# Filler products ahead of x, transposed blocks copied by ScalarE, and a later sum of blocks, in a hybrid attention layer on one core

## The chip, the core and the metric

The kernel runs on one core of a Trainium2 chip. The core has five engines, each with a queue of its own that it works off in order: TensorE (PE in the profile; its weight loads are listed apart as PEld), VectorE (DVE), ScalarE (ACT), GpSimd (POOL) and SyncE (SP), which here only issues DMAs. Matrix products leave their sums in one of eight PSUM banks of 128x512 numbers; everything else lies in SBUF or in device memory. Instructions wait for each other through semaphores. The metric is the device time of one execution in microseconds (us), the median of several runs.

## The reference

One layer: a norm of the input, one wide projection into nine parts, two groups of heads side by side, an output projection and a second norm.

```python
h = rms_norm(x, pre_g)                                  # x: 1024 x 1024
z = einsum('bsd,de->bse', h, w_in)                      # 7184 columns
qa, ka, va, ga, qb, kb, vb, gb, gk_low = split_columns(z)
# 8 heads: w = softmax(q1 k1^T) - lam * softmax(q2 k2^T), causal; oa = w v
oa = rms_norm(diff_attention(qa, ka, va, lam), subln_g) * (1 - lam_init) * silu(ga)
# 4 gated heads: S_t = diag(exp(log_a_t)) S_{t-1} + k_t^T v_t ; o_t = q_t S_t, in chunks
log_a = log_sigmoid(gk_low @ w_gk_up + b_gk) / 16
ob = rms_norm(gla_chunked(qb, kb, vb, log_a), gla_g) * silu(gb)
y = einsum('bse,ed->bsd', concatenate([oa, ob], -1), w_out)
return x + rms_norm(y, post_g)
```

All inputs and the output are float32.

## The kernel before

**Split numbers.** TensorE takes its operands in a shorter format (fp32r). Each operand is therefore split into a part `hi`, a rounded copy that ACT makes, and a part `lo`, the difference that DVE makes, and a product is three: hi by hi, hi by lo, lo by hi. So each block that TensorE is to use costs ACT one instruction and DVE one, and DVE comes last.

**Seven products for eight.** The normed input h is transposed and cut into a 2x2 grid of blocks, by tokens and by columns of x: `h11`, `h12` from the first 512 tokens, `h21`, `h22` from the last. A pair of projection columns is cut likewise into `b11` to `b22`. Seven block products then stand for eight. Products n = 1, 2 and 4 take the blocks h11, h12, h22; n = 5, 6, 7, 3 take the sums `s1` = h21 + h22, `s2` = s1 - h11, `s3` = h11 - h21 and `s4` = h12 - s2. In the code, `f1` holds whole copies of h11 and h12; s2 is written over the first, and s4 is taken from the second (`f1lo`) and the first (`f1hi`). Each block has four pieces j = 0..3 of 128x512. The weights of n = 5, 6, 4, 7 are differences of the b blocks, which DVE writes over the raw columns `w_raw`. One step (p, n) of the list `order` is one product for one pair of columns; `go(n)` issues the next n steps, and inside it `prepare` makes weights up to three steps ahead. Weights lie in a ring of five tiles, raw columns in four buffers: a load of new raw columns waits until the last reader of the old ones is done. A step leaves its sum in a bank named x, y or z, 24 products to a step in the first part.

**The start.** Eight 128-row tiles of x are loaded, the first four ahead. For each of these, ACT squares and sums it (`junk`), ACT and DVE work out the scale, DVE scales the first 512 columns and POOL the rest. `first(0)` transposes the first halves of the four tiles into four banks (`xT`), from which `put` makes h11; `first(1)` does it for h12. Tiles 4 to 7 are normed two at a time and scaled by POOL. `blocks(j)`, j = 0..3, transposes two more blocks of these and makes from them piece j of h22, s1, s2 and s3: ACT copies h21 and h22_hi out of the banks, and DVE reads the second bank twice more, for h22_lo and for s1. After them come four pieces of s4, four subtractions on DVE and their split. `low_rank` then prepares a small weight `wl2` and multiplies it with all blocks (`gkl_ps`); its gates are needed by later steps.

**Later.** The remaining steps of the projection run to the end of the list; between them the generator `gla(g)` places the work of the four gated heads, one piece at each `yield`: scores (`pa`, `pk`), states (`kv`), outputs (`gpo`), their sum of squares (`gms`), and the store. The last pairs (VALS) are the values of the attention heads; there two pieces are drawn to a step. Then come the attention heads, run against the output projection, and the end.

**What sets the order.** A scheduler of the framework orders each engine's queue by data and its own estimates, except where the code holds instructions in the order in which they are written (`keep_in_program_order`: every product and transpose, and some of the start) or ties them behind another (`issue_after`). Banks are handed out from a list `free`, oldest first; who takes a bank waits for its last readers.

The lines that the steps of the prediction touch are L117 (product), L120 (transpose), L333, L352 and L353 (weights: difference, hi, lo), L574 (squares), L604 and L605 (split from a bank), L623 and L625 (f1), L645 to L652 and L630, L631 (blocks), L721 (s4), L734 to L752 (low_rank), L462 (values).

## Time and profile before

| | us |
|---|---|
| median of 3 runs (lowest to highest) | 974.47 (974.18 to 975.09) |
| the profiled execution, its own time | 975.12 |
| its span, first to last instruction | 973.4 |
| TensorE busy | 952.3 (98%) |
| VectorE busy | 734.2 (75%) |
| ScalarE busy | 603.0 (62%) |
| GpSimd busy | 205.7 (21%) |

The profile is of one execution. The timeline gives for each group of like instructions the start, the busy time of the group, engine, line, operation, what it writes and reads, the shape and the count; a bracket at the end gives how long the engine stood idle before it, and what ended that. Instructions overlap at their ends, so the time that an engine gives to each is read from one start to the next and not from the busy time. Products are pipelined: 24 of the form 128x256 have busy times that overlap by much, and their rate is read from the starts. The table of stretches shows, after start:end and length, the busy time and count for PE, PEld, DVE, ACT and POOL, then the granted clock of TensorE and the traffic of the DMAs.

### The profile page before, as it was taken

What the parts mean: (1) busy time and instruction counts of PE and PEld (TensorE: products, weight loads), DVE (VectorE), ACT (ScalarE), POOL (GpSimd) and SP (SyncE); (2) the same over time, 40 slices, a digit from 0 to 9 for tenths busy, and PEclk for the clock granted to TensorE, in tenths of its full rate; (3) what the DMA queues carried; (4) which work ended last, traced back from release to release, by engine and by line L of the source; (5) the groups of instructions that cost most, each with busy time, mean ns of one, the idle gap of its engine ahead of it and who ended that gap; (6) DMA issues with size and microseconds to landing.
All of it is one profiled execution on the core that took longest, in us unless ns stands there. A gap on an engine that the chain in (4) does not pass through costs nothing.

```text
span 973.4 us, 15020 instructions
## 1 busy us (share of the span) xinstructions
PE 952.3 (98%) x4946; PEld 811.1 (83%) x4946; DVE 734.2 (75%) x1462; ACT 603.0 (62%) x1164; POOL 205.7 (21%) x263
## 2 busy tenths in 40 slices
PE   6999999999999999999999999999999999999997
PEld 5998988888888888888888888878888888888785
DVE  6887598897677686686766677487888888898554
ACT  8642454764667565576765344366786687887773
POOL 4300001212141221131100002121322222443322
PEclk9999999999999999999999999999999999999999
DMA  9443456478768987996854589997656759995777
GB/s 356 142 113 89 139 162 233 168 243 268 229 205 253 290 271 257 285 299 208 258 184 125 175 240 288 397 295 240 222 173 225 235 194 356 333 292 106 153 212 144
DMA packets 152301, 220.39 MB, mean 226 GB/s; under 512 B 16752, under 2 KB 87408, under 8 KB 152128
## 3 DMA queue, kind: packets, MB, share of 16 engines
q1 hardware_dynamic: 138128, 178.80, 57.5%
q0 software_dynamic: 14096, 40.64, 14.7%
q8 instruction: 39, 0.64, 0.3%
q14 instruction: 38, 0.31, 0.1%
HBM read 133.93 MB, written 88.60 MB: 229 GB/s over the span
## 4 chain that ended last, share of the span: by engine, by line
PE 93%; DVE 3%; ACT 1%; DMA 1%; issue 1%; POOL 0%; DVEq 0%; SPq 0%; ACTq 0%
PE x L117 24%; PE z L117 15%; PE y L117 14%; PE ypart L117 13%; PE sc L117 7%; PE po L117 5%; PE yps L117 4%; PE wtr L120 3%; PE gpo L117 3%; PE kv L117 1%; PE gkl_ps L117 1%; PE pa L117 1%; DMA v_raw<-in_w_in_dram 1%; PE xT L120 0%; ACT junk L574 0%
## 5 line engine op out<-in xcount | busy, mean ns | idle before, releaser
L352 ACT CAST w<-w_raw 128x512 fp32r<-128x512 f32 (+1 forms) x150 | 98.0, 655 | 90.1 <-PE y L117 46.9
L353 DVE TENSOR_TENSOR w<-w_raw,w 128x512 fp32r<-128x512 f32 (+1 forms) x150 | 109.4, 732 | 40.8 <-ACT w L352 40.4
L1148 ACT ACTIVATE p<-p,stt 128x896 f32<-128x896 f32 (+7 forms) x128 | 99.3, 777 | 36.5 <-DVE stt L1138 33.8
L510 ACT COPY s<-x 128x512 f32<-128x512 f32 x72 | 42.2, 586 | 74.7 <-PE x L117 74.2
L1154 POOL TENSOR_SCALAR p<-p,stt,lam 128x1024 f32<-128x1024 f32 (+3 forms) x64 | 56.2, 878 | 146.6 <-DVE stt L1153 144.9
L677 POOL DMA_DIRECT2D wo_d<-wo_hi x32 | 17.7, 552 | 328.6 <-ACT wo_hi L667 328.6
L1138 DVE CUSTOM_DVE_ANT_0 p<-sc,maskt 128x512 f32<-128x512 f32 (+3 forms) x128 | 74.3, 585 | 14.8 <-PE sc L117 13.5
L117 PE MATMUL z<-s_hi,w 128*128 128x512 f32 x320 | 80.2, 393 | 0.0
L117 PE MATMUL x<-s_hi,w 128*128 128x512 f32 x320 | 80.0, 392 | 0.0
L117 PE MATMUL y<-h_hi,w 128*128 128x512 f32 x320 | 80.0, 392 | 0.0
L117 PE MATMUL ypart<-wo_hi,m_hi 128*128 128x512 f32 x192 | 79.5, 414 | 0.1
L117 PE MATMUL ypart<-wo_hi,m_lo 128*128 128x512 f32 x192 | 75.5, 393 | 0.0
L117 PE MATMUL ypart<-wo_lo,m_hi 128*128 128x512 f32 x192 | 75.4, 393 | 0.0
L333 DVE TENSOR_TENSOR w_raw<-w_raw 128x512 f32<-128x512 f32 (+1 forms) x88 | 66.2, 752 | 9.3 <-DMA w_raw<-in_w_in_dram 8.2
L117 PE MATMUL sc<-k,q 128*128 128x512 f32 (+1 forms) x192 | 68.9, 363 | 1.2 <-DVE stt L1138 1.2
L117 PEld LDWEIGHTS z<-s_hi,w 128*128 128x128 f32 x320 | 59.7, 188 | 12.2
L117 PEld LDWEIGHTS y<-h_hi,w 128*128 128x128 f32 x320 | 59.7, 188 | 12.2
L117 PEld LDWEIGHTS x<-s_hi,w 128*128 128x128 f32 x320 | 59.7, 188 | 12.2
L117 PE MATMUL sc<-ks,q 128*128 128x512 f32 (+1 forms) x192 | 66.1, 347 | 0.0
L1196 ACT CAST wt_hi<-wtr 128x512 fp32r<-128x512 f32 (+1 forms) x80 | 42.8, 535 | 25.3 <-PE wtr L120 24.4
L1197 DVE TENSOR_TENSOR wt_lo<-wtr,wt_hi 128x512 fp32r<-128x512 f32 (+1 forms) x80 | 50.6, 633 | 9.1 <-ACT wt_hi L1196 8.4
L1157 DVE SCALAR_TENSOR_TENSOR p<-p,stt,p 128x1024 f32<-128x1024 f32 (+3 forms) x64 | 52.1, 814 | 4.1 <-POOL p L1154 3.8
(236 smaller groups left out, 2323.5 us busy)
## 6 DMA issues: line engine op xcount, KB each, us to landing
w_raw<-in_w_in_dram SPq DMA_DIRECT2D x48, 512.0 KB, 4.6
wo_d<-wo_hi POOLq DMA_DIRECT2D x32, 256.0 KB, 3.3
q<-q_d SPq DMA_DIRECT2D x32, 256.0 KB, 5.1
k<-k_d SPq DMA_DIRECT2D x32, 256.0 KB, 5.6
ks<-k_d SPq DMA_DIRECT2D x64, 128.0 KB, 6.0
v<-v_d SPq DMA_DIRECT2D x16, 512.0 KB, 7.1
wo_raw<-in_w_out_dram POOLq DMA_DIRECT2D x31, 256.0 KB, 4.9
wo_d<-gqd POOLq DMA_DIRECT2D x22, 256.0 KB, 4.1
```

The lines of the kernel that those rows point to most:

```text
L117: tc.keep_in_program_order(pe.matmul(*a, **k))
L120: tc.keep_in_program_order(pe.transpose(dst, src, ident))
L333: dve.tensor_tensor(dst, a, b, ALU.subtract)
L352: act.copy(w[0], src)
L353: dve.tensor_tensor(w[1], src, fp(w[0]), ALU.subtract)
L510: act.copy(b[k], ps)
L1138: ins = dve.tensor_tensor_reduce(p[:, a:e], sc[:, : e - a], maskt[:, NZ + P - (e - a) :] if last else maskt[:, : e - a], 1.0, 3e38 if i == ...
L1148: act.activation(p[:, :n], p[:, :n], AF.Exp, bias=st[:, m : m + 1], scale=-1.0, accum_out=st[:, 2 + m : 3 + m],)
L1154: pool.tensor_scalar(p1[:, :n], p1[:, :n], st[:, 5:6], lam, ALU.mult, ALU.mult)
L1157: dve.scalar_tensor_tensor(p0[:, :n], p0[:, :n], st[:, 4:5], p1[:, :n], ALU.mult, ALU.subtract)
L1196: act.copy(hi[:, :n], pt[:, :n])
L1197: dve.tensor_tensor(lo[:, :n], pt[:, :n], fp(hi[:, :n]), ALU.subtract)
```

## The change

Seven things are altered.

- The constants `ones` and a zeroed tile `idle` are made first on POOL. `spin(n)` multiplies the two n times into a bank that nobody reads. 14 such products stand ahead of the first transposes, and 3, 7, 3 and 4 behind the transposes of tiles 0 to 3.
- While `pinned` is set, ACT, DVE and POOL keep the written order too: it holds for the start, for the split of h11, for the norm of tiles 4 to 7, which is now written ahead of the first step, and for the copies of `blocks(0)`. The first four weights are tied by this in place of `issue_after`; weights 4 to n_early + 1 are tied behind the last pinned instruction.
- POOL's four additions for `f1[0]` come after the scaling of tiles 4 to 7.
- `blocks`: ACT copies h22 whole out of its bank into SBUF; hi, lo and s1 are made from that copy. The bank is read by ACT alone. For odd j the copy uses the buffer `t4`, which the first piece of w_out used from the start and now gets later.
- `blocks(j)` stands one step earlier among the steps, and s4 four steps later, its four subtractions tied behind DVE's latest instruction there.
- The multiplication of `sub_g` on DVE is held in the written order.
- In the last gated head's second half two of the three-`yield` delays are two `yield`s long.

```diff
@@ constants, queues
-    act, dve, pool, pe, sp = nc.scalar, nc.vector, nc.gpsimd, nc.tensor, nc.sync
+    pe, sp = nc.tensor, nc.sync
+    pinned = [False]
+
+    class Queue:
...
+            def run(*a, **k):
+                ins = op(*a, **k)
+                self.latest = getattr(ins, "ins", None)
+                if pinned[0]:
+                    tc.keep_in_program_order(ins)
+                    self.last = ins.ins
+                return ins
...
+    act, dve, pool = Queue(nc.scalar), Queue(nc.vector), Queue(nc.gpsimd)
...
+    ones = const.tile([P, P], F32R, name="ones")
+    pool.memset(fp(ones), 1.0)
+    idle = hw.tile([P, 512], F32R, tag="s1_hi0", name="idle")
+    pool.memset(fp(idle), 0.0)
...
-        if i < 4:
-
-            act_ins, dve_ins = normed[0][:2]
-            with tc.issue_after(act_ins.ins), tc.issue_after(dve_ins.ins):
+        if 4 <= i <= n_early + 1:
+            with tc.issue_after(act.last), tc.issue_after(dve.last):
                 make_weights(i)
...
+    spins = []
+
+    def spin(n):
+
+        if not spins:
+            spins.append(bank(free[-1], [P, 512], "spin"))
+        for i in range(n):
+            mm(spins[0], ones, idle, start=(i == 0), stop=(i == n - 1))
...
     def first(h):
 
         ps = [take_bank([P, 512], "xT") for _ in range(HB)]
+        if not h:
+            spin(14)
         for i in range(4):
             for j in range(HB):
                 k = h * HB + j
                 tr(ps[j][0][:, i * P : (i + 1) * P], xs[i][:, k * P : (k + 1) * P])
+            if not h:
+                spin((3, 7, 3, 4)[i])
         hi, lo = H[("h11", "h12")[h]]
         for j in range(HB):
             put(ps[j][0], h * HB + j, (hi, lo), j)
+        pinned[0] = not h
+        for j in range(HB):
             if h:
                 act.activation(f1[h][:, j], ps[j][0], AF.Copy, scale=pre_g[:, h * HB + j : h * HB + j + 1])
-            else:
-                pool.tensor_tensor(f1[h][:, j], fp(at(hi, j)), fp(at(lo, j)), ALU.add)
             free.append(ps[j][1])
...
         k = j + HB
+        pinned[0] = not j
         h21 = t_c("h21")
+        h22 = ap.tile([P, 512], F32, tag="t4", name="h22", bufs=1) if j % 2 else t2k("s", 4, "h22")
         act.activation(h21, pss[0], AF.Copy, scale=pre_g[:, j : j + 1])
-        put(pss[1], k, block("h22"), j)
+        act.activation(h22, pss[1], AF.Copy, scale=pre_g[:, k : k + 1])
         s1 = t_c("s1")
-        dve.scalar_tensor_tensor(s1, pss[1], pre_g[:, k : k + 1], h21, ALU.mult, ALU.add)
+        dve.tensor_tensor(s1, h21, h22, ALU.add)
+        pinned[0] = False
+        parts("h22", j, h22)
         parts("s1", j, s1)
...
-    prepare(0)
+    for i in range(4):
+        prepare(i)
     first(0)
-    for i in range(1, 4):
-        prepare(i)
+    norm_x(4, 5)
+    norm_x(6, 7)
+    for j in range(HB):
+        pool.tensor_tensor(f1[0][:, j], *(fp(at(part, j)) for part in H["h11"]), ALU.add)
     go(1)
     first(1)
     go(2)
-    norm_x(4, 5)
-    norm_x(6, 7)
-    go(1)
     for j in range(HB):
         blocks(j)
         go(1)
-    go(2)
+    go(3)
+    go(4)
     s4 = [kp.tile([P, 2, 512], F32, tag=f"k{i}", name="s4") for i in range(2)]
-    for j in range(HB):
-        dve.tensor_tensor(s4[j // 2][:, j % 2], f1[1][:, j], f1[0][:, j], ALU.subtract)
+    with tc.issue_after(dve.latest):
+        for j in range(HB):
+            dve.tensor_tensor(s4[j // 2][:, j % 2], f1[1][:, j], f1[0][:, j], ALU.subtract)
...
-    go(6)
+    go(2)
...
-            yield
-            yield
-            yield
+            last = g == GLA_HEADS - 1 and half == 1
+            for _ in range(2 if last else 3):
+                yield
...
-            yield
-            yield
-            yield
+            for _ in range(2 if last else 3):
+                yield
```

In the built program the queues stand as follows. First TensorE's own, from its first instruction to the first products of the projection (`x<-w,h_hi`), before:

```order
L120 MATMUL xT<-ident,x_185 128x128 x8
L120 MATMUL xT<-ident,x_188 128x128 x8
L117 MATMUL x<-w,h_hi 128x256 x16
L117 MATMUL x<-w,h_lo 128x256 x8
L120 MATMUL xT<-ident,x_185 128x128 x8
```

and now (a product is L142 here, a transpose L145):

```order
L142 MATMUL spin<-idle,ones 128x512 x14
L145 MATMUL xT<-ident,x_187 128x128 x4
L142 MATMUL spin<-idle,ones 128x512 x3
L145 MATMUL xT<-ident,x_187 128x128 x4
L142 MATMUL spin<-idle,ones 128x512 x7
L145 MATMUL xT<-ident,x_190 128x128 x4
L142 MATMUL spin<-idle,ones 128x512 x3
L145 MATMUL xT<-ident,x_190 128x128 x4
L142 MATMUL spin<-idle,ones 128x512 x4
L142 MATMUL x<-w,h_hi 128x256 x16
```

The fillers stand among the four tiles' transposes; what follows is in the order that it had.

Second, VectorE between the last weights of the first two pairs and the small weights of low_rank (`ku`, `wl2`). The numbers are those of buffers: w_799 is the lo part of the weights of step (0, 4), w_831 that of (0, 7), and w_793, 795, 827 are raw columns of pairs 2 and 3 that are newly loaded, each into a buffer that one of these weights was read from. Before:

```order
L353 TENSOR_TENSOR w_799<-w_raw_194,w_798 128x1024
L631 TENSOR_TENSOR s4_lo_757<-s4_750,s4_hi_756 128x512 x2
L631 TENSOR_TENSOR s4_lo_757<-s4_751,s4_hi_756 128x512 x2
L353 TENSOR_TENSOR w_831<-w_raw_204,w_830 128x1024
L333 TENSOR_TENSOR w_raw_793<-w_raw_795,w_raw_793 128x1024
L333 TENSOR_TENSOR w_raw_795<-w_raw_827,w_raw_795 128x1024
L454 TENSOR_TENSOR gv_st_944<-z_768,s_942 128x512
```

and now, where nearly every instruction bears the line of the class Queue (L66), and the same buffers are 823, 855, 817, 819 and 851:

```order
L66 TENSOR_TENSOR w_823<-w_raw_196,w_822 128x1024
L66 TENSOR_TENSOR s2_lo_509<-f1hi_257,s2_hi_507 128x512
L66 TENSOR_TENSOR w_raw_817<-w_raw_819,w_raw_817 128x1024
L66 TENSOR_TENSOR w_855<-w_raw_206,w_854 128x1024
L66 TENSOR_TENSOR s4_910<-f1lo_258,f1hi_257 128x512 x2
L66 TENSOR_TENSOR s4_911<-f1lo_258,f1hi_257 128x512 x2
L66 TENSOR_TENSOR w_raw_819<-w_raw_851,w_raw_819 128x1024
L66 TENSOR_TENSOR s4_lo_917<-s4_910,s4_hi_916 128x512 x2
L66 TENSOR_TENSOR s4_lo_917<-s4_911,s4_hi_916 128x512 x2
L66 CAST ku_927<-gk_up_997 16x512 x2
```

The first difference of newly loaded columns moved ahead of the second weights and of s4; the split of s4 moved behind both differences.

Third, TensorE in the last gated head, between its `gpo` products and the third step of the values (`z`). Before, `gpo` stands behind the second value step `x`, and then:

```order
L117 MATMUL y<-w,h_hi 128x512 x8
L117 MATMUL y<-w,h_lo 128x512 x8
L117 MATMUL y<-w,h_hi 128x512 x16
L117 MATMUL y<-w,h_lo 128x512 x8
L117 MATMUL y<-w,h_hi 128x512 x8
L117 MATMUL gms<-sq_hl,ones 128x512 x2
L117 MATMUL z<-w,s_hi 128x512 x8
```

Now `gpo` stands ahead of that step `x`, and then:

```order
L142 MATMUL y<-w,h_hi 128x512 x8
L142 MATMUL y<-w,h_lo 128x512 x8
L142 MATMUL y<-w,h_hi 128x512 x8
L142 MATMUL gms<-sq_hl,ones 128x512 x2
L142 MATMUL y<-w,h_hi 128x512 x8
L142 MATMUL y<-w,h_lo 128x512 x8
L142 MATMUL y<-w,h_hi 128x512 x8
L142 MATMUL z<-w,s_hi 128x512 x8
```

`gpo` and `gms` each moved ahead by one step of 24 products.

More of the change, by code (lines that the diff above doesn't have):

```diff
@@ L53, in hymba_kernel, with __init__, __getattr__ @@
     nc = tc.nc
-    act, dve, pool, pe, sp = nc.scalar, nc.vector, nc.gpsimd, nc.tensor, nc.sync
+    pe, sp = nc.tensor, nc.sync
+    pinned = [False]
+    class Queue:
+        def __init__(self, engine):
+            self.engine = engine
+        def __getattr__(self, name):
+            op = getattr(self.engine, name)
+            def run(*a, **k):
[5 more added lines that the diff above has]
+                return ins
+            return run
+    act, dve, pool = Queue(nc.scalar), Queue(nc.vector), Queue(nc.gpsimd)
     def fp(t):
@@ L60, in cols @@
         return slice(half * 512, half * 512 + 512)
+    edge = ctx.enter_context(tc.tile_pool(name="edge", bufs=1, side="right"))
+    hw = ctx.enter_context(tc.tile_pool(name="hw", bufs=1, side="right", reuse_waits="tile"))
     const = ctx.enter_context(tc.tile_pool(name="const", bufs=1))
+    ones = const.tile([P, P], F32R, name="ones")
+    pool.memset(fp(ones), 1.0)
+    idle = hw.tile([P, 512], F32R, tag="s1_hi0", name="idle")
+    pool.memset(fp(idle), 0.0)
+    pool.memset(edge.tile([P, 120], F32, name="edge"), 0.0)
     pre_g = const.tile([P, KT], F32, name="pre_g")
@@ L68, in hymba_kernel @@
     pool.memset(eps_t, EPS)
-    ones = const.tile([P, P], F32R, name="ones")
-    pool.memset(fp(ones), 1.0)
     NZ = 512
@@ L120, in tr @@
         tc.keep_in_program_order(pe.transpose(dst, src, ident))
-    edge = ctx.enter_context(tc.tile_pool(name="edge", bufs=1, side="right"))
-    pool.memset(edge.tile([P, 120], F32, name="edge"), 0.0)
-    hw = ctx.enter_context(tc.tile_pool(name="hw", bufs=1, side="right", reuse_waits="tile"))
     hpool_cm = tc.tile_pool(name="hpool", bufs=1, side="right")
```

14 lines of the change are left out of this document (6 added, 8 removed).

## The prediction

> **What bounds the kernel now.** I read the page first, then TensorE's waits, then the stretches, then the timeline where TensorE waits.
>
> ```profile
> span 973.4 us, 15020 instructions
> PE 952.3 (98%) x4946; PEld 811.1 (83%) x4946; DVE 734.2 (75%) x1462; ACT 603.0 (62%) x1164; POOL 205.7 (21%) x263
> ...
> PE xT L120 <- DVE x L565: 9.0, 4, 7.6
> PE y L117 <- DVE s L648: 1.3, 1, 1.3
> ...
> PE z L117 <- DVE c L462: 1.1, 1, 1.1
> PE y L117 <- ACT s L510: 0.7, 1, 0.7
> ...
> 13.80:19.60 5.80, 5.78 (x25) 5.55 (x26) 5.66 (x8) 5.80 (x11) 3.82 (x3) 1.00 1.05 395
> 41.00:59.00 18.00, 16.58 (x116) 15.21 (x115) 17.86 (x27) 9.25 (x15) 0.80 (x2) 1.00 0.14 42
> ```
>
> TensorE bounds the kernel: it is busy for 98% of the span, so only what lets it start sooner, run faster or wait less can count. Its waits (total, times, longest) are few: 9.0 us for x at the start, 1.3 us for s1, 1.1 us for the values, 0.7 us for a bank that ACT reads. The two stretches (PE, PEld, DVE, ACT, POOL, then the clock) warn of a second limit: from 41 to 59 us DVE is busy for 17.86 of 18.00 us. What TensorE gains ahead of that it keeps only as far as DVE lets it.
>
> The start of TensorE:
>
> ```profile
> 7.56 1.09 PE L120 MATMUL xT<-ident,x 128*128 128x128 f32 x4 [7.56 <-DVE x L565]
> ...
> 13.82 4.24 PE L117 MATMUL x<-w,h_hi 128*128 128x256 f32 x16 [0.38 <-ACT h_hi L604]
> 17.85 1.88 PE L117 MATMUL x<-w,h_lo 128*128 128x256 f32 x8
> 19.56 1.92 PE L120 MATMUL xT<-ident,x 128*128 128x128 f32 x16
> ...
> 24.19 2.08 PE L117 MATMUL y<-w,h_hi 128*128 128x256 f32 x16
> 26.11 1.12 PE L117 MATMUL y<-w,h_lo 128*128 128x256 f32 x8
> ```
>
> Eight h_lo products take from 17.85 to 19.56, 0.214 us each; 16 of the same size take 24.19 to 26.11, 0.12 us each. So the first step runs at near half rate, though the stretch above gives a granted clock of 1.00: that column doesn't show this.
>
> **The fillers.** They need two memsets on POOL; the second is like this one:
>
> ```profile
> 30.54 0.53 POOL L734 MEMSET ku<- 128x512 f32 x1 [1.17 <-DVE w L353]
> 9.60 1.04 ACT L574 ACTIVATE junk<-x 128x1024 f32<-128x1024 f32 x1
> 11.20 1.98 ACT L352 CAST w<-w_raw 128x1024 fp32r<-128x1024 f32 x2
> 13.09 2.42 ACT L604 ACTIVATE h_hi<-xT,pre_g 128x512 fp32r<-128x512 f32 x4
> 14.95 2.71 DVE L605 SCALAR_TENSOR_TENSOR h_lo<-xT,pre_g,h_hi 128x512 fp32r<-128x512 f32 x4
> 15.38 1.07 ACT L574 ACTIVATE junk<-xt 128x1024 f32<-128x1024 f32 x1
> ```
>
> Work begins near 0.8 us, so fillers can run from about 1.6. No row shows one; by the rates above a 512-wide product is 0.43 us at the low rate and 0.24 at the full one. Fourteen last to between 5.0 and 7.6, and the first x is ready at 7.56: cost 0 to 0.1. If the rate is full by then, seven fillers (1.7) put tile 2's transposes off by some 0.5 us, from 10.7 to 11.2, three (0.7) let tile 3's start at 12.4 for 12.3; nothing is lost, since ACT casts weights until 13.09 and only then copies h_hi. The first product stays at 13.82. Is the rate full? Steady products began at 13.82 and the 16 transposes at 19.56 took 0.1 us each, so at most 5.7 us of steady work are needed; from 1.6 that ends at 7.4. I take full.
>
> The first step then goes with its inputs: h_lo's last piece is done at 17.66, and with two products of 0.12 the step ends near 18.0 instead of 19.56: 1.56 us earlier. This gain has a cover on it. ACT now takes all four squares and both scale chains before it copies h12: from 15.38 a square (1.03), a square with its chain (1.60, from 9.60 to 11.20), again both, one copy of 0.5: h_hi of h12 near 21.15. Before it was 21.19, waiting for transposes. ACT is late in TensorE's place, and TensorE loses part of the gain in step (0, 2): by pieces I get 25.7 for its end against 27.07, 1.4 us earlier.
>
> [...] Of the stretch from 7.5 to 13.8 the trace can say only that 16 transposes alone had not brought the full rate.
>
> **Blocks through ACT.** The rows that DVE's pace is read from, one start to the next:
>
> ```profile
> 23.48 1.07 ACT L352 CAST w<-w_early 128x1024 fp32r<-128x1024 f32 x1
> ...
> 60.60 1.22 DVE L353 TENSOR_TENSOR w<-w_raw,w 128x1024 fp32r<-128x1024 f32 x1
> 61.74 2.49 DVE L631 TENSOR_TENSOR s_lo<-s,s_hi 128x512 fp32r<-128x512 f32 x4
> 61.89 3.91 SPq L195 DMA_DIRECT2D w_raw<-in_w_in_dram  x2
> 64.15 1.22 DVE L353 TENSOR_TENSOR w<-w_raw,w 128x1024 fp32r<-128x1024 f32 x1
> 65.83 1.23 DVE L333 TENSOR_TENSOR w_raw<-w_raw 128x1024 f32<-128x1024 f32 x1 [0.46 <-DMA w_raw<-in_w_in_dram]
> 69.26 1.23 DVE L333 TENSOR_TENSOR w_raw<-w_raw 128x1024 f32<-128x1024 f32 x1 [2.21 <-DMA w_raw<-in_w_in_dram]
> 70.41 0.68 DVE L454 TENSOR_TENSOR gv_st<-z,s 128x512 f32<-128x512 f32 x1
> 75.53 0.29 DVE L746 TENSOR_TENSOR wl<-wd,wl 128x128 fp32r<-128x128 f32 x1
> 76.28 1.99 PE L117 MATMUL gkl_ps<-h_hi,wl 128*64 128x512 f32 x8
> ```
>
> The bank's last reader is now ACT, so the 1.3 us wait for DVE's s1 goes. What is late next there is ACT's copy of block 2, near 37.7, for which step (2, 2) waits 0.2 us. Four more casts on ACT (0.55 each) lie beside DVE's work. DVE itself saves next to nothing: an instruction of 512 costs it 0.60 us (four from 61.74 to 64.15), from a bank hardly more.
>
> DVE's start into this region: ACT's weight cast at 23.45, as before, one copy (0.5), four of f1lo (0.57 each, as h_hi from 13.09 to 15.38), two blocks (0.65 each): the first s1 at 28.6. From there by the new order up to the lo weights of step (0, 4) stand 34 instructions of 0.60 and 8 of 1.14 (60.60 to 61.74), each with its input there in time: 29.5 us. The weights end at 58.1; before, they ended at 61.74. This is not the 1.4 us of the start: it is s4's four subtractions (2.4) gone from here, against two differences and one value sum that came in.
>
> **Where it is paid back.** In the new order the difference of the newly loaded columns follows next but one. Their load waits for those lo weights, by the old rows 61.89 to 65.83, 3.94 us. So DVE, which before split s4 meanwhile (61.74), now stands idle from 58.7 until 62.1. Behind it are the lo weights of step (0, 7), which end at 64.4 (before: 64.15 + 1.22), and whose buffer the next load waits for: its difference comes 3.9 us later, 68.3, against 69.26. s4's subtractions fit between; its split, 4 x 0.60 = 2.4, does not, and now follows. Then the same instructions as before from 70.41 to the small weights' lo part, end 75.82: 5.4 us. Sum: 68.3 + 1.14 + 2.4 + 5.4 = 77.3. The product that waits for it, gkl_ps, began at 76.28 before without a wait. TensorE would be there at 74.4: step (0, 6) ends behind DVE's last split of s2 (58.7) at 59.1, (1, 6) at 62.0, then four steps of 24 x 0.12 = 2.9 and ACT's bank wait of 0.7 to 0.8. It waits 3 us, and begins at 77.4. POOL, once it has scaled tiles 4 to 7 (from 18.6 on), adds f1 from 24 to 30 us now, beside DVE, which has shown longer rows under that:
>
> ```profile
> 15.78 6.06 POOL L625 TENSOR_TENSOR f1hi<-h_hi,h_lo 128x512 f32<-128x512 f32 x4 [2.95 <-DVE h_lo L605]
> 20.61 2.31 DVE L333 TENSOR_TENSOR w_raw<-w_raw 128x1024 f32<-128x1024 f32 x1
> ...
> 23.95 5.41 POOL L565 TENSOR_SCALAR xt<-xt,ssq 128x1024 f32<-128x1024 f32 x4 [2.12 <-ACT h_hi L604]
> ```
>
> against 1.2 for its like: 0 to 1.1 us more. I take 0.3, because most rows beside POOL keep their 0.6: gkl_ps at 77.7, **1.4 us later than before** (0.8 to 2.2). From there to 533 us TensorE has no wait in the trace, and the order is the same: the loss stays.
>
> **The last gated head.**
>
> ```profile
> 518.15 0.38 PE L117 MATMUL gpo<-gan,gv 128*128 128x128 f32 x2
> ...
> 521.63 2.07 PE L117 MATMUL y<-w,h_hi 128*128 128x512 f32 x8
> ...
> 529.01 1.28 DVE L462 TENSOR_TENSOR c<-y,s 128x512 f32<-128x512 f32 x2
> ...
> 533.07 0.40 PE L117 MATMUL z<-w,s_hi 128*128 128x512 f32 x1
> 533.87 1.28 DVE L462 TENSOR_TENSOR c<-y,s 128x512 f32<-128x512 f32 x2
> ...
> 534.60 1.89 PE L117 MATMUL z<-w,s_hi 128*128 128x512 f32 x7 [1.14 <-DVE c L462]
> ```
>
> The second z product waited for the bank of the y just ended: 534.60 - 533.07 less a product of 0.23 is 1.3 us. Now gpo (3.5 us) and gms come earlier, gms takes a bank between the two y steps, and the hand-out shifts by one: the second y step wants the first one's bank. That is read by DVE 0.6 us after the step's end, of which gms (0.46) and one product cover all but 0.3; the z step gets banks long free. **Gain 1.0** (0.3 to 1.3). sub_g on DVE, and the first piece of w_out, which on SP's queue now stands behind eight stores of values, are needed only a hundred us on and more: 0. The fillers' bank is next written by TensorE itself: 0.
>
> **Sum.** +1.4 - 1.0 = +0.4 us: 975.5 against the profiled 975.12 (span 973.4 and 1.7 around it), which lies 0.65 above the median. On the median: **974.9**, its own range 974.0 to 976.4.
>
> **Rivals.** *Faster, 971.6.* DVE is ready for gkl_ps before TensorE is, at 74.4; then gkl_ps begins 1.9 us earlier and with the 1.0 the change brings 2.9 us. It decides where the chain from the first s1 is 3 us shorter than I count. For it: most of DVE's and ACT's order here is my reading of one trace, and 42 rows of it. Against: the two loads alone hold 7.8 us of it.
> *Slower, 978.4: fillers of zeros don't bring the full rate, so they don't do what they are for.* At 0.43 us 31 of them and 16 transposes (0.2) last from 1.6 to 18; ACT gets the last tile's transposes at 16.6 for 13.09, all behind moves by 3.5, and 974.9 becomes 978.4. It decides if the rate is still low at 9 us. Against it: steady products did bring it by 19.56.
> *Slower, 977.* POOL's f1 slows all of DVE's first rows (28.6 to 30) as at 20.61: 1.5 to 2 us more on the chain.
> *The full rate lapses again between the tiles,* where fillers fill 3.9 of 6.3 us: the first step is back at 19.56, but ACT's 21.15 hides all but some 0.3 of it, since DVE's chain starts there: 975.2. [...]
>
> **Chances.** My case 0.61, the lapse 0.05, the faster rival 0.20, the fillers 0.06, POOL 0.08. Of the first two 0.60 stay within 0.2% (1.95 us, about what a measurement can tell), 0.04 end above, 0.02 below. So faster 0.22, same 0.60, slower 0.04 + 0.06 + 0.08 = 0.18. The range, 971.4 to 977.0, leaves out what of the faster rival ends below its 971.6 (0.08, if DVE gains more yet) and the fillers.
>
> **What would show it.** Steps of 24 products at 0.12 us from the first (right) or 0.21 (fillers wrong); no wait for s1; DVE idle some 3 us near 60 for w_raw; a wait of TensorE near 75 for DVE's wl, about 3 us; at 530 a wait of 0.3 in place of 1.1. I am wrong if that wl wait is missing, or if another stands between 80 and 530 us.

## The result, and the profile after

The changed kernel is slower: 978.27 us (median of 6 runs, 978.15 to 978.78) against 974.40 (6 runs), ratio 1.0035, interval 1.0025 to 1.0045. The profiled execution took 978.19 us, its span is 976.5. The forecast was 974.9, the range 971.4 to 977.0.

TensorE's waits now (where the time was waited for; total, times, longest):

```profile
PE y L142 <- ACT s L66: 2.8, 1, 2.8
PE spin L142 <- POOL idle L66: 1.5, 1, 1.5
PE sc L142 <- DVE stt L66: 1.4, 2, 0.8
PE x L142 <- DVE s_lo L66: 0.8, 1, 0.8
PE x L142 <- ACT h L66: 0.6, 1, 0.6
PE gkl_ps L142 <- DVE wl L66: 0.5, 1, 0.5
```

Of the 9.0 us for x 0.2 are left (the fillers run there now, behind 1.5 us for their own operand `idle`); the 1.3 for s1 and the 1.1 for the values are gone. New are two short waits ahead of 61 us (0.6 and 0.8), one of 2.8 us for ScalarE, where 0.7 stood before, and 0.5 us in front of gkl_ps, where there was none. The timeline of TensorE shows what this did (start, busy time, ...; in brackets the idle time ahead and what ended it):

```profile
16.74 1.38 PE L142 MATMUL x<-w,h_lo 128*128 128x256 f32 x8
17.95 1.91 PE L145 MATMUL xT<-ident,x 128*128 128x128 f32 x16
...
25.77 1.03 PE L145 MATMUL xT<-ident,xt 128*128 128x128 f32 x8
...
63.24 2.08 PE L142 MATMUL y<-w,h_hi 128*128 128x256 f32 x16
...
71.95 3.50 PE L142 MATMUL y<-w,h_hi 128*128 128x256 f32 x16 [2.79 <-ACT s L66]
75.29 1.11 PE L142 MATMUL y<-w,h_lo 128*128 128x256 f32 x8
...
79.78 2.03 PE L142 MATMUL gkl_ps<-h_hi,wl 128*64 128x512 f32 x8 [0.51 <-DVE wl L66]
81.65 2.00 PE L142 MATMUL gkl_ps<-h_lo,wl 128*64 128x512 f32 x8
```

Before, the step that now waits 2.79 us had this wait:

```profile
70.42 2.18 PE L117 MATMUL y<-w,h_hi 128*128 128x256 f32 x16 [0.68 <-ACT s L510]
```

Set against the same instructions before, the lag (after less before) is the ledger of the change:

| the instruction | before | after | lag |
|---|---|---|---|
| end of the first step | 19.56 | 17.95 | -1.61 |
| step (0, 4) | 63.82 | 63.24 | -0.58 |
| step (1, 4) | 70.42 | 71.95 | +1.53 |
| gkl_ps | 76.28 | 79.78 | +3.50 |
| first value step z | 533.07 | 537.13 | +4.06 |
| first value step x after it | 545.41 | 548.01 | +2.60 |
| end of the span | 973.4 | 976.5 | +3.1 |

So 1.6 us are gained at the start, all of it and 3.5 us more are lost by gkl_ps, 0.5 us are lost little by little up to 533 us, and the last gated head gives 1.46 back. Between 548 us and the end 0.5 us are lost again, 0.35 of it at one score product near 817 us. TensorE's waits for VectorE ahead of the scores come to 1.1 to 2.8 us in the profiles of the runs below, so this part differs from run to run.

VectorE at the loss:

```profile
58.15 1.23 DVE L66 TENSOR_TENSOR w<-w_raw,w 128x1024 fp32r<-128x1024 f32 x1
59.28 0.70 DVE L66 TENSOR_TENSOR s_lo<-f1hi,s_hi 128x512 fp32r<-128x512 f32 x1
64.39 1.23 DVE L66 TENSOR_TENSOR w_raw<-w_raw 128x1024 f32<-128x1024 f32 x1 [4.41 <-DMA w_raw<-in_w_in_dram]
65.53 1.22 DVE L66 TENSOR_TENSOR w<-w_raw,w 128x1024 fp32r<-128x1024 f32 x1
66.66 2.49 DVE L66 TENSOR_TENSOR s<-f1lo,f1hi 128x512 f32<-128x512 f32 x4
70.66 1.23 DVE L66 TENSOR_TENSOR w_raw<-w_raw 128x1024 f32<-128x1024 f32 x1 [1.51 <-DMA w_raw<-in_w_in_dram]
71.81 2.49 DVE L66 TENSOR_TENSOR s_lo<-s,s_hi 128x512 fp32r<-128x512 f32 x4
...
79.35 0.29 DVE L66 TENSOR_TENSOR wl<-wd,wl 128x128 fp32r<-128x128 f32 x1
```

It stands idle for 4.41 us at a load, does the lo weights of (0, 7) late, stands idle at the next load, then splits s4, and only then makes the small weights. From 70.66 to 79.6 it has no idle time. And ScalarE, which holds the bank at 70 us:

```profile
63.44 0.59 ACT L66 COPY s<-x 128x512 f32<-128x512 f32 x1 [2.28 <-PE x L142]
65.70 1.06 ACT L66 CAST w<-w_raw 128x1024 fp32r<-128x1024 f32 x1 [1.67 <-DVE w_raw L66]
69.25 2.18 ACT L66 CAST s_hi<-s 128x512 fp32r<-128x512 f32 x4 [2.49 <-DVE s L66]
71.33 0.57 ACT L66 COPY s<-x 128x512 f32<-128x512 f32 x1
```

The sums of s4 end at 69.1, so their four casts run from 69.25 and the copy of the sum of step (0, 7), ready at 69.0, comes behind them. After the wait TensorE's next 16 products last from 71.95 to 75.29, 0.21 us each, in place of 0.12. Here the granted clock (last but two of the columns) does show it:

```profile
72.00:73.50 1.50, 1.50 (x7) 1.50 (x8) 1.50 (x3) 0.00 (x0) 0.00 (x0) 0.50 0.05 11
73.50:75.30 1.80, 1.80 (x12) 1.80 (x12) 1.74 (x5) 0.00 (x0) 0.00 (x0) 0.59 0.00 0
75.30:77.00 1.70, 1.70 (x17) 1.70 (x16) 1.67 (x5) 0.56 (x1) 0.00 (x0) 1.00 0.19 67
```

Two theories, then. **A:** VectorE's chain sets gkl_ps: the waits for the two loads put the small weights at 79.6, and what TensorE lost at 70 us it would have lost at gkl_ps. **B:** ScalarE's casts ahead of the copy are the cause: 2.8 us of wait and 1.4 us of half rate, 4.2 in all.

### The profile page after: what moved, and what is told of

It is laid out like the page before. It is cut to its first block, busy times and chain, and to the rows that moved or that the text cites. A ratio compares the mean times of both kernels' runs of the same rounds, so it can differ in the third digit from the quotient of the medians.

```text
span 976.5 us, 15095 instructions
## 1 busy us (share of the span) xinstructions
PE 960.7 (98%) x4977; PEld 816.3 (84%) x4977; DVE 734.9 (75%) x1462; ACT 605.6 (62%) x1168; POOL 205.1 (21%) x264
## 4 chain that ended last, share of the span: by engine, by line
PE 89%; DVE 4%; DMA 3%; issue 2%; SPq 1%; ACT 0%; POOL 0%; DVEq 0%; ACTq 0%; POOLq 0%
PE x L142 21%; PE z L142 15%; PE y L142 14%; PE ypart L142 13%; PE sc L142 7%; PE po L142 5%; PE yps L142 4%; PE wtr L145 3%; PE gpo L142 3%; PE kv L142 1%; DMA w_early<-in_w_in_dram 1%; DMA w_raw<-in_w_in_dram 1%; PE gkl_ps L142 1%; PE pa L142 1%; DVE s_lo L66 1%
## 5 line engine op out<-in xcount | busy, mean ns | idle before, releaser
L66 ACT CAST w<-w_raw 128x512 fp32r<-128x512 f32 (+1 forms) x150 | 98.2, 656 | 95.4 <-PE y L142 49.1
L66 DVE TENSOR_TENSOR w<-w_raw,w 128x512 fp32r<-128x512 f32 (+1 forms) x150 | 109.7, 733 | 45.3 <-ACT w L66 44.8
L66 ACT ACTIVATE p<-p,stt 128x896 f32<-128x896 f32 (+7 forms) x128 | 99.3, 777 | 36.7 <-DVE stt L66 35.0
L66 ACT COPY s<-x 128x512 f32<-128x512 f32 x84 | 48.9, 586 | 91.0 <-PE x L142 90.5
L66 POOL DMA_DIRECT2D wo_d<-wo_hi x32 | 17.6, 550 | 331.2 <-ACT wo_hi L66 331.2
L66 POOL TENSOR_SCALAR p<-p,stt,lam 128x1024 f32<-128x1024 f32 (+3 forms) x64 | 56.0, 875 | 147.2 <-DVE stt L66 142.4
L66 DVE CUSTOM_DVE_ANT_0 p<-sc,maskt 128x512 f32<-128x512 f32 (+3 forms) x128 | 74.3, 585 | 14.7 <-PE sc L142 13.4
L142 PE MATMUL z<-s_hi,w 128*128 128x512 f32 x320 | 80.2, 393 | 0.0
L142 PE MATMUL x<-s_hi,w 128*128 128x512 f32 x320 | 80.1, 392 | 0.0
L142 PE MATMUL y<-h_hi,w 128*128 128x512 f32 x320 | 80.0, 392 | 0.0
L142 PE MATMUL ypart<-wo_hi,m_hi 128*128 128x512 f32 x192 | 79.5, 414 | 0.1
L66 DVE TENSOR_TENSOR w_raw<-w_raw 128x512 f32<-128x512 f32 (+1 forms) x88 | 66.3, 753 | 12.4 <-DMA w_raw<-in_w_in_dram 11.3
L142 PE MATMUL ypart<-wo_hi,m_lo 128*128 128x512 f32 x192 | 75.5, 393 | 0.0
L142 PE MATMUL ypart<-wo_lo,m_hi 128*128 128x512 f32 x192 | 75.4, 393 | 0.0
L142 PE MATMUL sc<-k,q 128*128 128x512 f32 (+1 forms) x192 | 69.0, 363 | 1.5 <-DVE stt L66 1.4
L142 PEld LDWEIGHTS y<-h_hi,w 128*128 128x128 f32 x320 | 59.7, 188 | 12.3
L142 PEld LDWEIGHTS z<-s_hi,w 128*128 128x128 f32 x320 | 59.7, 188 | 12.3
L142 PEld LDWEIGHTS x<-s_hi,w 128*128 128x128 f32 x320 | 59.7, 188 | 12.3
L142 PE MATMUL sc<-ks,q 128*128 128x512 f32 (+1 forms) x192 | 66.0, 347 | 0.0
L66 ACT CAST wt_hi<-wtr 128x512 fp32r<-128x512 f32 (+1 forms) x80 | 42.8, 534 | 25.1 <-PE wtr L145 24.3
L66 DVE TENSOR_TENSOR wt_lo<-wtr,wt_hi 128x512 fp32r<-128x512 f32 (+1 forms) x80 | 50.6, 633 | 8.9 <-ACT wt_hi L66 8.3
L66 DVE TENSOR_TENSOR c<-z,s 128x512 f32<-128x512 f32 x48 | 32.9, 689 | 31.6 <-ACT s L66 20.0
```

The costliest lines, as they stand in the source:

```text
L66: ins = op(*a, **k)
L142: tc.keep_in_program_order(pe.matmul(*a, **k))
```

## The experiments

Each ratio is to the kernel before on the same chip, with its 95% interval; that kernel's median there was 974.40 to 975.10 us, so a tenth of a per cent is about 1 us. gkl_ps begins at 76.28 us before and at 79.78 after. Three of the kernels leave something out of the layer: no_loads has wrong weights in five products, f1_by_dma and f1_left_out lack the lo part of h11 in three sums.

| kernel | ratio | interval | gkl_ps begins | its wait |
|---|---|---|---|---|
| after | 1.0035 | 1.0025 to 1.0045 | 79.78 | 0.5 |
| s4_cast_later | 1.0059 | 1.0045 to 1.0072 | 79.79 | 3.9 |
| s4_late | 1.0007 | 0.9998 to 1.0016 | 77.05 | 1.1 |
| no_loads | 0.9987 | 0.9978 to 0.9996 | 75.85 | 0 |
| w07_first | 1.0005 | 0.9996 to 1.0014 | 76.38 | 0.4 |
| f1_left_out | 0.9994 | 0.9985 to 1.0003 | 75.69 | 0.5 |
| f1_by_dma | 1.0104 | 1.0090 to 1.0117 | 85.25 | 0.3 |
| no_fillers | 1.0031 | 1.0020 to 1.0042 | 79.44 | 1.8 |
| before_fillers | 1.0037 | 1.0024 to 1.0050 | 79.89 | 0 |
| wl_early | 0.9998 | 0.9989 to 1.0007 | 75.79 | 0 |
| wl_early_ones | 0.9995 | 0.9986 to 1.0004 | 75.78 | 0 |
| wl_ones_no_fillers | 0.9996 | 0.9987 to 1.0004 | 76.09 | 0 |
| delays_only | 0.9990 | 0.9981 to 0.9999 | 76.43 | 0 |

### ScalarE's casts or VectorE's chain

```diff
@@ s4_cast_later
-    for j in range(HB):
-        parts("s4", j, s4[j // 2][:, j % 2])
...
     go(2)
+    with tc.issue_after(act.latest):
+        for j in range(HB):
+            parts("s4", j, s4[j // 2][:, j % 2])
```

> The changed kernel with ScalarE's four casts of s4 tied behind its copy of the sum of step (0, 7), so that they no longer stand ahead of it; VectorE's work up to the small weights stays the same. Theory A (gkl_ps is set by VectorE's chain through two loads): TensorE no longer waits 2.8 us at 70 us, reaches gkl_ps near 75.6 and waits there near 3.9 us until 79.5, no gain: 978.3, and 979.7 if products after such a wait run at half rate there too. Theory B (the casts ahead of the copy are the cause, 2.8 us of wait and 1.4 us of half rate behind it): both go, 974.1.

The wait at 70 us falls to 0.7, and TensorE reaches gkl_ps 3.4 us earlier (75.88 for 79.27), only to wait there:

```profile
74.76 1.12 PE L142 MATMUL x<-w,s_lo 128*128 128x256 f32 x8
79.79 2.93 PE L142 MATMUL gkl_ps<-h_hi,wl 128*64 128x512 f32 x8 [3.91 <-DVE wl L66]
82.52 2.71 PE L142 MATMUL gkl_ps<-h_lo,wl 128*64 128x512 f32 x8
85.06 2.08 PE L142 MATMUL z<-w,s_hi 128*128 128x256 f32 x16
```

gkl_ps begins at 79.79, to a hundredth where it began with the casts in the way. On VectorE the four splits of s4 stand among other instructions now, but all still ahead of the small weights. Theory B is out. The kernel even loses 2.3 us to the changed one (ratio 1.0059): the half rate now falls on gkl_ps, whose 16 products last from 79.79 to 85.06, 5.27 us, in place of 3.70. That is 1.6 of the 2.3; the rest is lost behind 627 us, in the attention part. The long wait at 70 us was the cheaper place for it, as the time lost there was lost anyway.

```diff
@@ s4_late, all of s4 into low_rank
     go(4)
-    s4 = [kp.tile([P, 2, 512], F32, tag=f"k{i}", name="s4") for i in range(2)]
...
         go(2)
+        s4 = [kp.tile([P, 2, 512], F32, tag=f"k{i}", name="s4") for i in range(2)]
...
         for half in range(2):
```

> The changed kernel with all of s4 (subtractions, casts, split) behind the first two steps of low_rank, so behind the small weights on VectorE and behind the copies on ScalarE. Theory A: VectorE's chain loses the split of 2.4 us, the small weights are ready near 77.0, gkl_ps begins near 77.3 behind a wait of 1.7: 975.8, and 977.2 if that wait already brings the half rate. Theory B: 974.1, with no wait over 1 us between 60 and 80.

Ratio 1.0007. Theory A's 975.8 against 974.4 is 1.0014 and lies inside the interval; theory B's 974.1, 0.9997, lies just outside. The trace decides: the small weights are done at 76.8 and gkl_ps begins at 77.05, after a wait of 1.1; its 16 products run at the full rate.

### The loads

```diff
@@ no_loads, in fetch_raw
-                load_raw(2, (0,))
-                load_raw(3, (0,))
+                raws[2] = {0: raws[0][0]}
+                raws[3] = {0: raws[0][1]}
             elif n == 7:
-                load_raw(3, (1,))
+                raws[3][1] = raws[1][0]
...
             if n == 5:
-                load_raw(2, (1,))
+                raws[2][1] = raws[1][1]
```

> The changed kernel without the four loads of raw columns for pairs 2 and 3: these take what pairs 0 and 1 left in the same four buffers, so five products of the second group have wrong weights, and nothing else differs; s4 stays where the change put it, its casts ahead of the copy too. Theory A (VectorE's chain is long because it waits 4.4 and 1.5 us for these loads): the small weights are ready near 75.3, TensorE waits for them 0.5 us at most and no longer for 2.8 us at 70: 4 us less than the changed kernel, equal to the kernel before within 0.8. If the loads are not the cause: 3.4 us above the kernel before, as the changed kernel.

Ratio 0.9987: 4.7 us less than the changed kernel, and 1.3 less than before, where 4 and at most 0.8 were expected; in the traces 4.0 of it lie ahead of 627 us, the rest in the attention part. Both large waits are gone with the loads, ScalarE's too (0.7 us at 70), and gkl_ps begins at 75.85 without one. So the waits for these loads are the cause; whether it is the loads' length or what stands behind the wait for them, this tells:

```diff
@@ w07_first: one tie in prepare(i)
+    w07 = []
...
+        elif i == 18:
+            with tc.issue_after(w07[0]):
+                make_weights(i)
         else:
             make_weights(i)
+            if i == 15:
+                w07.append(dve.latest)
```

> The changed kernel with one tie: VectorE's difference of the newly loaded columns (for step (2, 5)) comes behind the lo weights of step (0, 7), as in the kernel before; s4 stays where the change put it, its casts ahead of the copy too. Theory A (the chain is long because the difference that waits for its load stands ahead of the weights that free the next load's buffer): these weights run near 62.3, when their ring tile is free, in place of 65.53; the second load goes 3 us earlier, the small weights are ready near 76.5, gkl_ps begins near 76.7 in place of 79.78: 3 us less than the changed kernel, 0.5 to 1 above the kernel before. If the loads' own length is the cause and not what stands behind the wait: no more than 1 us less than the changed kernel.

Ratio 1.0005: 3 us less than the changed kernel, with one instruction tied behind another. VectorE there:

```profile
59.34 0.68 DVE L66 TENSOR_TENSOR s_lo<-f1hi,s_hi 128x512 fp32r<-128x512 f32 x1
62.59 1.23 DVE L66 TENSOR_TENSOR w<-w_raw,w 128x1024 fp32r<-128x1024 f32 x1 [2.57 <-issue]
63.73 2.49 DVE L66 TENSOR_TENSOR s<-f1lo,f1hi 128x512 f32<-128x512 f32 x4
66.14 1.22 DVE L66 TENSOR_TENSOR w_raw<-w_raw 128x1024 f32<-128x1024 f32 x1
67.28 0.68 DVE L66 TENSOR_TENSOR s_lo<-s,s_hi 128x512 fp32r<-128x512 f32 x1
67.88 1.22 DVE L66 TENSOR_TENSOR w_raw<-w_raw 128x1024 f32<-128x1024 f32 x1
```

and SyncE's two loads (start and time until both are issued), of the changed kernel, then of w07_first:

```profile
59.44 7.71 SPq L217 DMA_DIRECT2D w_raw<-in_w_in_dram  x2
```

```profile
59.49 4.73 SPq L217 DMA_DIRECT2D w_raw<-in_w_in_dram  x2
```

The lo weights of (0, 7) run at 62.59 in place of 65.53, so the second load is out 3 us earlier and runs beside the first one's wait; neither difference has to wait. The tie has also let s4's four subtractions and one of its splits in ahead of the differences. The casts of s4 are still ahead of ScalarE's copy, and TensorE waits 0.8 us at 70. With this one tie 3.4 of the 3.5 us at gkl_ps are gone.

### GpSimd beside VectorE

```diff
@@ f1_by_dma
-        pool.tensor_tensor(f1[0][:, j], *(fp(at(part, j)) for part in H["h11"]), ALU.add)
+        act.dma_start(f1[0][:, j], fp(at(H["h11"][0], j)))
```

> The changed kernel with GpSimd's four additions for f1 of h11 left out; the buffer is filled with h_hi alone by four DMAs on ScalarE's queue instead, so s2, s3 and s4 lack the lo part of h11. Theory A with GpSimd in VectorE's way: VectorE's first s1 and the difference behind it take 0.6 and 1.14 us for 0.86 and 2.23, the chain ends 1.35 us earlier and gkl_ps with it: 1.2 us less than the changed kernel (1.0 to 1.5), 2.2 above the kernel before. If GpSimd does not slow VectorE, the two rows keep their length and the time is the changed kernel's.

This didn't measure what it was for. ScalarE computed nothing for 6.3 us ahead of h12: 2.7 until it issued the first of the DMAs at 23.61, and 3.6 while it issued the four. The profile names the copy of x to the output, a DMA of another queue, as what ended the wait; why the first DMA was so late stays open:

```profile
23.61 3.56 ACTq L66 DMA_DIRECT2D f1hi<-h_hi  x4
27.21 0.59 ACT L66 COPY s<-x 128x512 f32<-128x512 f32 x1 [6.31 <-DMA out_dram<-in_x_dram]
```

TensorE waited 5.5 us for h12, gkl_ps began at 85.25, and the time says nothing on GpSimd.

```diff
@@ f1_left_out
-    for j in range(HB):
-        pool.tensor_tensor(f1[0][:, j], *(fp(at(part, j)) for part in H["h11"]), ALU.add)
...
-        dve.tensor_tensor(h21, h11, h21, ALU.subtract)
-        dve.tensor_tensor(h11, s1, h11, ALU.subtract)
+        hi11 = fp(at(H["h11"][0], j))
+        dve.tensor_tensor(h21, hi11, h21, ALU.subtract)
+        dve.tensor_tensor(h11, s1, hi11, ALU.subtract)
```

> The changed kernel without GpSimd's four additions for f1 of h11; s3 and s2 are taken from h11's hi part alone, which lacks its lo part. VectorE's order up to the lo weights of step (0, 4) keeps its instructions, a few change places; the lo weights of (0, 7) come ahead of the first loaded difference. Theory A with GpSimd in VectorE's way: the first s1 and the difference behind it last 0.60 and 1.14 us in place of 0.86 and 2.23, and the lo weights of (0, 4) end near 58.0 in place of 59.28; the loads then go earlier and gkl_ps with them, 976.7 on the clock of the changed kernel's 978.3 (2.3 above the kernel before). If GpSimd does not slow VectorE: both rows keep their length, and the weights end at 59.3.

The first VectorE rows of the blocks, of the changed kernel, with GpSimd adding until 30.5 us:

```profile
28.41 0.93 DVE L66 TENSOR_TENSOR s<-h,h 128x512 f32<-128x512 f32 x1 [1.42 <-ACT h L66]
29.27 2.30 DVE L66 TENSOR_TENSOR w_raw<-w_raw 128x1024 f32<-128x1024 f32 x1
31.50 0.68 DVE L66 TENSOR_TENSOR h<-f1hi,h 128x512 f32<-128x512 f32 x1
```

and of f1_left_out:

```profile
28.47 0.69 DVE L66 TENSOR_TENSOR s<-h,h 128x512 f32<-128x512 f32 x1 [1.74 <-ACT h L66]
29.08 1.22 DVE L66 TENSOR_TENSOR w_raw<-w_raw 128x1024 f32<-128x1024 f32 x1
30.21 0.68 DVE L66 TENSOR_TENSOR h<-h_hi,h 128x512 f32<-128x512 f32 x1
```

From one start to the next the two instructions take 0.86 and 2.23 us beside GpSimd and 0.61 and 1.13 without it: 1.35 us. The chain keeps it: the same 43 instructions from the first s1 on take 31.47 us in the changed kernel and 30.14 here. The time is another matter: 974.08, 4 us less than the changed kernel where 1.6 were expected, because in this kernel's order the lo weights of (0, 7) stand ahead of the first loaded difference, which the expectation named but gave no price. The run is w07_first and the GpSimd edit in one, and only the rows above speak for GpSimd alone.

### The fillers

```diff
@@ no_fillers
-        if not h:
-            spin(14)
...
-            if not h:
-                spin((3, 7, 3, 4)[i])
```

> The changed kernel without its 31 filler products. Theory A (DVE's chain sets gkl_ps): the first step falls back to 0.21 us a product and ends near 19.5 instead of 17.95, but ScalarE's first copy of h12, at 21.04 now, moves only to 21.2, so 0.2 us are lost: 978.5. Rival (what the fillers gain reaches the end): 1.6 us lost, 979.9. If the fillers do harm by anything that the trace does not show, below 978.0.

Ratio 1.0031, the changed kernel's within its interval; the eight times lie from 977.04 to 979.76, so the trace has to say more. The first step ends at 19.38 (19.56 in the kernel before), ScalarE's copies of h12 begin at 21.16 for 21.04, VectorE's first s1 comes at 28.81 for 28.41, and by 45 us, at step (4, 1), the lag to the changed kernel is down from 1.43 to 0.17 us (44.94 and 44.77).

> wl_early_ones without its 31 fillers: what they are worth where the loads no longer hold TensorE back. Theory A: the first step ends at 19.4, the lag is gone by 60 us but for the 0.4 us by which VectorE's first s1 comes later (28.8 for 28.4), 0.4 more than wl_early_ones at most. Rival: with no wait at 70 to 80 us left to hide it, the whole 1.4 us come back, 975.4.

This kernel is wl_early_ones (below) less the same lines. 0.9996 against 0.9995, gkl_ps at 76.09 against 75.78: the fillers are worth 0.3 us there, not 1.4, since TensorE, starting later, waits less for VectorE and ScalarE (1.0 us at 54 in place of 0.6 and 0.8 at 45 and 60).

```diff
@@ before_fillers: the kernel before, with
...
+    idle = hw.tile([P, 512], F32R, tag="s1_hi0", name="idle")
+    pool.memset(fp(idle), 0.0)
...
+        if not h:
+            spin(14)
...
+            if not h:
+                spin((3, 7, 3, 4)[i])
```

> The kernel before with the two memsets and the 31 fillers, nothing else. The first step ends near 18.0 in place of 19.56. Theory A: TensorE then waits for what ScalarE and VectorE make of h12, of the later tiles and of the blocks, as before, so gkl_ps begins at most 0.3 us earlier than 76.28 and the time is that of the kernel before within 0.4. Rival: the 1.5 us of the first step stay to the end, 972.9.

Neither came: 3.6 us slower than before. (In this edit the memsets of `ident`, `eps_t` and `edge` move behind the two, as in the changed kernel.) The scheduler, whose order is not held in that kernel, now put the first square of tile 4 between the first copy of h_hi and the other three, and tiles 4 to 7 were scaled later:

```profile
15.36 2.62 PE L121 MATMUL x<-w,h_hi 128*128 128x256 f32 x14 [1.11 <-ACT h_hi L614]
...
31.22 0.33 PE L124 MATMUL xT<-ident,xt 128*128 128x128 f32 x1 [1.68 <-POOL xt L575]
32.31 0.77 PE L124 MATMUL xT<-ident,xt 128*128 128x128 f32 x5 [0.77 <-POOL xt L575]
32.84 3.29 PE L121 MATMUL x<-w,h_hi 128*128 128x256 f32 x16
```

Two waits close together, and the 16 products behind them at 0.19 us. In the changed kernel, whose order at the start is held ("pinned"), the fillers do no such harm, and they don't make it faster. That holding the order is what keeps them harmless is argued from these two kernels; no run holds the order alone.

### Repairs

```diff
@@ wl_early
     go(3)
-    go(4)
+    gk_up = t_c("gk_up")[:R]
+    sp.dma_start(gk_up, w_gk_up[0])
+    wd = t_c("wd").rearrange("p (k r) -> p k r", r=R)
...
+    sp.dma_start(wl, w_in[0, :, GKL : GKL + GK_RANK].rearrange("(k p) c -> p k c", p=P))
+    go(3)
...
+    wl2 = kp.tile([P, KT + HB, 64], F32R, tag="q0", name="wl2")
...
+    go(1)
...
         go(2)
+        held = dve.latest
+        with tc.issue_after(held):
...
+            dve.tensor_copy(up[0:R], gk_up)
...
+        s4 = [kp.tile([P, 2, 512], F32, tag=f"k{i}", name="s4") for i in range(2)]
+        with tc.issue_after(held):
+            for j in range(HB):
+                dve.tensor_tensor(s4[j // 2][:, j % 2], f1[1][:, j], f1[0][:, j], ALU.subtract)
```

> The changed kernel with the small weights of low_rank loaded ahead of the raw columns and prepared while VectorE waits for the first load, and with s4 and the other small preparations (ku) behind the first two steps of low_rank. Theory A: gkl_ps waits for nothing and begins when TensorE gets there, near 75.8 against 76.28 before; with 0.9 from the last gated head (measured alone) 1.4 us less than the kernel before, 4.8 less than the changed kernel. If something else binds next, a wait of over 0.5 us between 76 and 95 us shows it.

The step that was foreseen came: no wait for VectorE in front of gkl_ps, which begins at 75.79. The time is 974.84 against 975.08, 3.6 us less than the changed kernel and level with the one before; 1.4 less was hoped for. Its profiled execution is 1.39 us ahead of the kernel before at 627 us (the first `ypart` product) and loses 0.65 of it near 654 us, where a score product waits 0.52 us for a load of `ks`; the profile of delays_only has such a wait too, that of the kernel before has none.

```diff
@@ wl_early_ones: wl_early, and
+    pre_g = const.tile([P, KT], F32, name="pre_g")
+    ident = const.tile([P, P], F32, name="ident")
+    eps_t = const.tile([P, 1], F32, name="eps_t")
     ones = const.tile([P, P], F32R, name="ones")
```

> As wl_early, with the tile of ones at the place in SBUF that it has in the kernel before. In the changed kernel's trace each of the eight gms pairs with the step behind it takes 0.05 us longer than before. If the tile's place does it: 0.4 us less than wl_early, each pair 0.46 us apart from the step behind it in place of 0.48. If not: equal to wl_early within 0.2.

A pair of gms products and what follows, of wl_early, then of wl_early_ones:

```profile
309.46 0.64 PE L142 MATMUL gms<-sq_hl,ones 128*128 128x512 f32 x2
309.94 2.02 PE L142 MATMUL y<-h_hi,w 128*128 128x512 f32 x8
```

```profile
309.39 0.62 PE L142 MATMUL gms<-sq_hl,ones 128*128 128x512 f32 x2
309.85 2.00 PE L142 MATMUL y<-h_hi,w 128*128 128x512 f32 x8
```

The pair is 0.46 us apart from its follower again, in place of 0.48, and the follower is 0.02 shorter. From gkl_ps to the first value step z TensorE takes 456.97 us with the tile at its old place (in this kernel as in delays_only, below) and 457.35 to 457.36 in the changed kernel and s4_late: 0.4 of the 0.56 us lost between 80 and 533 us hang on where in SBUF the tile lies. (The edit puts `pre_g`, `ident` and `eps_t` back too; `gms` reads none of these.) The medians are 0.9 us apart, more than this, and the intervals of the ratios overlap.

```diff
@@ delays_only: the kernel before, with
-            yield
-            yield
-            yield
+            last = g == GLA_HEADS - 1 and half == 1
+            for _ in range(2 if last else 3):
+                yield
...
-            yield
-            yield
-            yield
+            for _ in range(2 if last else 3):
+                yield
```

> The kernel before with the last gated head's two delays at 2 yields, nothing else. Prediction on record: the values' wait of 1.1 us goes but for 0.3, 1.0 us gained: 973.4. Read from the trace after, where TensorE waits nowhere between 520 and 545 us and the lag to before falls from 4.06 to 2.60 us over the last head: 1.46 gained, 972.9. Rival: the earlier gms and gpo only move the wait to another bank, 974.4.

Ratio 0.9990: 0.9 us faster, the interval just clear of one. It is the only part of the change that is shown to gain (ScalarE's copies of the blocks were not measured alone), and of the kernels here that compute the whole layer the only one shown to beat the kernel before.

## Why the prediction was wrong, point by point

- **The first step.** Right: full rate from the first product (one lasts 0.31 us there on average, 0.45 before and 0.28 in later steps; from start to start 16 take 3.03, since they go as h_hi comes), end at 17.95 (18.0 forecast), step (0, 2) ends at 25.77 (25.7). The fillers themselves show when the rate changed: they start 0.43 us apart up to 6.39 us and 0.24 apart from 6.77 on; that is ahead of the 7.4 us that the prediction took from the steady products of the kernel before. In before_fillers the first 14 last 5.59 us in place of 5.87, so the change comes earlier there. The rivals on the fillers' rate are out, the lapse between the tiles too.
- **The cover on it.** Right, and no_fillers shows it: what the start gains, ScalarE's and VectorE's chains give back.
- **The banks.** Right: the wait for s1 is gone; VectorE's first s1 came at 28.41 (28.6).
- **The term "1.4 us later than before" for gkl_ps** is the step that failed; it measured 3.50. Its mechanism is the one that the runs show, the difference of the loaded columns ahead of the lo weights whose buffer the next load needs (no_loads, w07_first), and its count of 34 and 8 instructions is what the trace has. Two of its sizes were wrong. GpSimd beside VectorE was taken as 0.3 and is 1.35; with the start 0.2 earlier, the lo weights of (0, 4) ended at 59.28 for 58.4. The first load was taken as 3.94 us, from the one row before; the difference began 5.11 us after those weights, 1.1 more than was counted. Together 2.0, and 77.7 became 79.78. Why that load took longer stays open: it lies beside other transfers (two of `k_d`, issued from 58.27 us on), it took 4.65 and 4.77 us in s4_late and wl_early, and no run isolated it.
- **Where TensorE waits.** Wrong: 3 us were forecast at gkl_ps, where 0.5 came; 2.8 came two steps earlier, behind four casts of s4 on ScalarE. That these casts, too, move behind the copy's place in ScalarE's queue was not looked at, since the 2.4 us were sought on VectorE alone. It cost nothing in the end (s4_cast_later). Nor was the half rate behind a wait of 3 us given a term: in s4_cast_later, where the wait stands where the prediction had it, it costs 1.6. That it is not in the changed kernel's sum is luck, since the casts moved the wait to where VectorE's chain hides it.
- **The last gated head.** The mechanism was right, the size was 1.0 and is 1.46 in the trace: the 48 products of the z steps last 10.88 us now and 12.34 before, so the wait had cost 1.46 and not 1.3, and of the 0.3 that were to be left at the second y step nothing is seen. Counted from the last `kv` product on, where the head's new order first costs some 0.15, 1.3 is left, here and in the trace of delays_only. Measured alone it gives 0.9.
- **Zero for the memsets.** They cost nothing themselves, but making `ones` first also moved its place, 0.4 us.
- **The range** ended at 977.0. It held GpSimd's part as a rival instead of my own sum's upper bound, though both can happen, and did: 974.9, 1.0 for GpSimd and 1.1 for the load make 977.0, and 0.5 between gkl_ps and the values (0.4 of it from `ones`) and 0.5 in the attention part less 0.46 of the head 977.5. The rest, 0.7, is the step from the profiled execution to the median: the one before lay 0.65 above its median, the one after 0.1 below, so the difference of the two spans, 3.1, is that much less than that of the medians, 3.9.

## What to carry to other kernels

Where an engine's queue order changes, look first for an instruction that waits for a load and stands ahead of one that frees the buffer of the next load: the two loads then ran one after the other here (7.71 us until both were issued, 4.73 in w07_first), and every later entry of that queue paid for both, 3.4 us at gkl_ps. Of two waits in a row the earlier can hide the later; take the later engine's chain to its end before you repair the earlier wait, since the repair alone may be worth nothing, or less (s4_cast_later lost 2.3 us more). A part that starts an engine earlier is worth only what the slowest chain behind it lets through: of the 1.4 us that the fillers gain at the start 0.3 are left at gkl_ps in wl_early_ones.

## What the runs showed of the hardware

**TensorE ran at half rate after the longer waits.** Waits of 1.08, 1.81 and 2.28 us (s4_late, no_fillers twice) were followed by products at the full rate, the first two by 16 of gkl_ps in 3.70 us, the last by 16 of a step in 2.02. Waits of 2.49 (f1_by_dma, 16 in 3.47 us), 2.79 (the changed kernel, 16 in 3.34), 3.91 (s4_cast_later, 16 of gkl_ps in 5.27) and 5.47 us (f1_by_dma, 16 in 4.04 where the first step of the changed kernel takes 3.03) were followed by half rate, for 3.3 us in the changed kernel, which costs another 1.4 to 1.6; so were the 1.68 and 0.77 of before_fillers with one transpose between them (16 in 3.08). The granted clock shows it (0.50 and 0.59 in the changed kernel, 0.51 in f1_by_dma, 0.60 in before_fillers), other than at the start of the kernel before, where the column gives 1.00 for products at 0.21 us. In these executions waits of 2.49 and 2.79 us were enough; 2.28 was not enough in the one execution that shows it. Whether the length alone sets it, no run tells.

**GpSimd's additions slow VectorE.** The delay was 1.35 us over two instructions whose inputs both lie in SBUF; the same form was slow in the kernel before (2.31 us at 20.61). The lo weights at 24.44, beside the same additions, took 1.95 us in the changed kernel and 1.23 in f1_left_out; `gv_st` at 26.32, which reads a bank and a tile, kept its length, 0.68 and 0.69.

**The place of a small constant in SBUF** changed a pair of products from 0.46 us (wl_early_ones) to 0.48 (wl_early); one of them lasts 0.392 us in the kernel before and 0.403 in the changed one. Why is open.
